# Packed matrix products recorded as one unit, and a mode-change charge in the order of the work

## The chip, the cores and the metric

One core of a Trainium2 chip runs the whole program. Its engines are TensorE (PE in the profile, PEld its weight loads), VectorE (DVE), ScalarE (ACT), GpSimdE (POOL, idle here) and SyncE (SP), which issues the transfers. The metric is the device time of one execution in microseconds (us), the median of several runs.

## What is computed

Two models one after the other on 256 tokens of width 1024, all in fp32, for one sequence. Cut to the parts around the change:

```python
def mixer_layer(...):                       # first block, 2 layers
    proj = h @ w_in
    ...                                     # 4 diff heads, 6 dilated heads, 6 forgetting heads
    s = einsum('bhmqd,bhmkd->bhmqk', qblk, k) * scale      # diff: two maps m per head, 32 wide
    p = softmax(where(causal, s, -inf))
    a = p[:, :, 0] - lam * p[:, :, 1]
    oa = einsum('bhqk,bhkd->bhqd', a, v)
    ...
def hybrid_layer(...):                      # second block, 2 layers
    ...                                     # 6 neighbourhood heads, 6 latent (MLA) heads, a convolution
    x = x + expert_choice_moe(rms_norm(x, norm_ffn), ...)
def expert_choice_moe(...):                 # 16 experts, 32 tokens each
    hid = silu(xs @ w_gate) * (xs @ w_up)
    ys = (hid @ w_down) * gate
    return zeros.at[bidx, idx].add(ys)
```

Each layer of the first block also has six modulation vectors (silu(c) @ w_mod), an output projection and a gated feed-forward stage with a width-3 convolution.

## The kernel before, in words

**Order of the work.** Nothing is issued where it is written. Every engine call is recorded by `Program.note` and `record` (lines 182 to 255) as one operation with its operands, a cost in ns (`cost`, 155) and its dependences. `order` (378) then makes a list schedule: `schedule` (257) keeps a list of ready operations per engine, sorted by rank, and again and again issues the one that can start first; of those that can start at the same time, the one of lower rank. Six forward rounds alternate with backward ones, and the round with the smallest modelled makespan is issued by `issue` (404), line 409: that is why every row of the profile names L409, and why rows are told apart by tile names. All operations that go through `either` (187) may run on VectorE or ScalarE, as the schedule finds better. Transfers keep their recorded order.

**The TensorE model.** For an operation on PE `record` notes its lanes, the 32-column strips of the array that its output covers (lines 211 to 213). An operation starts no earlier than its lanes are free; it then blocks its own lanes for its cost, and the engine itself for 20 ns. So the model knows that products in different column strips run side by side. It knows nothing of rows: two products that use different halves of the array's rows cover all four strips, and stand one behind the other in the model. Nor does it know any price for going from one shape of array use to another.

**Weights.** All weights stream through a ring of 16 buffers of 1 MiB (`ring`), filled by SP in one fixed sequence; a buffer is refilled when its last reader is done. A dense projection (`proj`, 801) splits each 512 weight columns into a rounded part (`whi`) and a rest (`wlo`) on VectorE or ScalarE, and takes three single-pass products for each 128x128 block: `ps<-h,whi` twice, `ps<-h,wlo` once. Everything else is plain fp32, which takes two passes: one product stands in the trace as two MATMUL records.

**Small products.** These do not fill the array:

- `modulation` (940): for each of 8 blocks k, four products of 32 output rows each, `ps<-ring,sct 128*32`. Seven of the twelve modulations run on VectorE instead (`ON_VECTOR`).
- `causal_scores` (988): for two query blocks b and two maps i, contraction over 64 rows, `ps<-kb,kb 64*128`. The forgetting heads add a row product with `pick6`.
- `attend` (1021): the probabilities are transposed on TensorE, then multiplied by the values of one or two heads, 64 output rows each, `ps<-kb,kb 128*64`.
- `soft_pair` (1257): the same for neighbourhood heads (64 rows) and latent heads (full rows).
- the experts (1575 to 1617): gate, up and down products of 32 output rows in groups of four, `ps<-ring,kb 128*32`, and eight products that scatter the result back, contraction over 32 rows, `ps<-kb,kb 32*128`, into four accumulators `yj`.

In the diff attention of `first_layer` (lines 1107 to 1126) the two maps passed to one `causal_scores` are those of the same head: q[0] and q[1] and the key all lie on partitions p0 to p0+63, with the other map's half zeroed. `attend` is called for one head at a time, with an offset that selects the half of `po`.

PSUM has eight buffers, all under the tag `ps`; the scores, sums, transposes and accumulators share them.

Of the kernel before, what the change touches and what calls it, by code (L numbers as in the profile page):

```python
# [21 lines left out]
NE = 16  # L22
# [16 lines left out]
class View:  # L39
    """A tile, or a view of one, that is allocated when the first instruction on it is issued."""  # L40
# [67 lines left out]
class Chunk:  # L108
    """Columns of a weight matrix that lie in several tiles."""
# [26 lines left out]
class Program:  # L136
    """Records instructions in the order of the data flow and issues them in the order in which a list
    scheduler finds their operands ready and their buffers free; the recorded order is the priority."""
# [5 lines left out]
    ROUNDS, PREFER, WAIT = 6, 3000.0, 1.0  # L144

    def __init__(self):
        self.ops, self.bufs, self.options = [], {}, None
        self.exp_ops, self.silu_ops, self.load, self.patience = [], [], None, 0.0

# [44 lines left out]
    def record(self, options):  # L194
        op = Op(index=len(self.ops), users={}, options={}, patience=self.patience)
        for engine, call, name, args, kw in options:
# [9 lines left out]
            op.options[engine] = call, args, kw, self.cost(engine, name, outs, ins, kw)  # L206
        op.engine = engine if len(options) == 1 else None
        op.cost, op.lag = min(o[3] for o in op.options.values()), max(self.LAG[e] for e in op.options)
        if engine == "PE":
            m = outs[0].shape[0]  # L210
            m = 32 if m <= 32 else 64 if m <= 64 else 128
            op.lanes = [0, 1, 2, 3][outs[0].part // m * m // 32:][:m // 32]
            op.columns = math.prod(outs[0].shape[1:]) * ins[0].shape[0] / 128 * len(op.lanes) / 4 * (
                2 if name == "transpose" else 1 if ins[0].dt == F32R else 4)
# [12 lines left out]
        func = args[2] if name == "activation" and op.engine else None  # L227
# [29 lines left out]
    def schedule(self, ops, rank, back=False):  # L257
        """A list schedule of the instructions, of which ops is an order that the buffers allow, or one
        of the reversed program."""
# [38 lines left out]
        lane = [0.0] * 4  # L298
        oldest, out = 0, []
        while len(out) < count:  # L300
# [3 lines left out]
            for e, ready in engines.items():  # L304
                found, tried = None, 0
                for r, i in ready:
# [39 lines left out]
            if e == "PE":  # L346
# [4 lines left out]
                columns += o.columns  # L351
            end = clock[e] = t + cost
# [50 lines left out]

    def issue(self):
        def real(a):
            return a.get() if isinstance(a, View) else a

        for o in self.order():
            o.ins = o.call(*[real(a) for a in o.args], **{k: real(v) for k, v in o.kw.items()})  # L409
# [251 lines left out]
def hybrid_kernel(ctx: ExitStack, tc: tile.TileContext, A, out, taps=None):  # L661
# [278 lines left out]
    def modulation(l, r):  # L940
# [15 lines left out]
        for k in range(8):  # L956
            for j in range(4):
# [30 lines left out]
    def causal_scores(q, k, mask, fneg=None, ftok=None, heads=None):  # L988
        sp = [sps(), sps()]
        for b in (1, 0):  # L990
            n = 128 * (b + 1)
            o = 128 * b
            for i in range(2):
                PE.matmul(sp[i][:, o:o + n], q[i][:, b * 128:(b + 1) * 128], k[i][:, :n],
                          start=True, stop=fneg is None)
            if fneg is not None:
                for i in range(2):
                    s = slice(64 * i, 64 * i + 38)
                    PE.matmul(sp[i][:, o:o + n], pick6[s, heads + i:heads + i + 1].to_broadcast([38, 128]),
                              fneg[s, :n], start=False, stop=True)  # L1000
# [20 lines left out]
    def attend(maps, vs, po, off=0):  # L1021
        parts = []
        for i, (full, low) in enumerate(maps):
# [7 lines left out]
            parts.append((slice(off + 64 * i, off + 64 * i + 64), t0, t1))  # L1031
# [28 lines left out]
    def first_layer(l, squares, following):  # L1060
# [46 lines left out]
        for c in range(2):  # L1107
            po = ops()[:, :256]
            for hh in range(2):
                p0 = 64 * hh  # L1110
                q = [qk[c][m][p0:p0 + 64] for m in range(2)]
                k = [qk[2 + c][p0:p0 + 64]] * 2
                dst, r4 = causal_scores(q, k, cf[:, C_CAU:C_CAU + 256])
                V.tensor_scalar(r4[:, 1:4:2], r4[:, 1:4:2], lam[:, l:l + 1], None, op0=ALU.mult)
                for b in range(2):
                    a0, a1 = dst[2 * b][0], dst[2 * b + 1][0]
                    scaled(a0, a0, r4[:, 2 * b:2 * b + 1])
                    V.scalar_tensor_tensor(a0, a1, r4[:, 2 * b + 1:2 * b + 2], a0, op0=ALU.mult, op1=ALU.add)
                attend([(dst[2][0], dst[0][0])], lambda b, i: vhead(2 * c + hh)(b, 0), po, p0)
# [137 lines left out]
    def soft_pair(q, k, v, bias, rq=None):  # L1257
        sp = [sps(), sps()]
        for b in range(2):
            for i in range(2):  # L1260
                PE.matmul(sp[i][:, b * 256:(b + 1) * 256], q[i][:, b * 128:(b + 1) * 128], k[i],
                          start=True, stop=True)
# [33 lines left out]
        for j in range(2):  # L1296
            for i in range(2):
                PE.matmul(po[64 * i:64 * i + 64, :], v(j, i), pT[i][j], start=(j == 0), stop=(j == 1))
# [13 lines left out]
    def second_layer(l, squares):  # L1312
# [262 lines left out]
        for e in range(NE):  # L1575
# [6 lines left out]
            for h, wx in enumerate((wg, wu)):  # L1582
                for k in range(8):
                    for j in range(4):
                        o = k * 1024 + j * 256
                        PE.matmul(gu[32 * j:32 * j + 32, h * 256:(h + 1) * 256], xe[k], wx[:, o:o + 256],
                                  start=(k == 0), stop=(k == 7))
# [17 lines left out]
            for kk in range(8):  # L1605
                for j in range(4):
                    o = kk * 1024 + j * 256
                    PE.matmul(po[32 * j:32 * j + 32, :256],
                              hT[:, (kk % 2) * 128 + 32 * (kk // 2):(kk % 2) * 128 + 32 * (kk // 2) + 32],
                              wd[:, o:o + 256], start=(kk == 0), stop=(kk == 7))  # L1610
            ys = kb()
            copy(ys, po[:, :256])
            for j in range(4):
                for c in range(2):
                    PE.matmul(yj[j][:, c * 256:(c + 1) * 256], ys[32 * j:32 * j + 32, c * 128:(c + 1) * 128],
                              gT[32 * j:32 * j + 32], start=(e == 0 and c == 0), stop=(e == NE - 1 and c == 1),
                              skip_group_check=True)
# [33 lines left out]
```

## Time and profile before

| | us |
|---|---|
| runs | 1908.0, 1904.19, 1908.54 |
| median of the runs | 1908.0 |
| profiled execution, first to last instruction (span) | 1906.3 |
| median above the span | 1.7 |

The page gives no other time for the profiled execution than its span. Read it by stages: the first block runs from 0 to about 706 us, the mixer of the second block's first layer from there to 857, its experts to 1299, the second layer's mixer to 1457, its experts to the end.

### The profile page before, as it was taken

To read this page: it belongs to the slowest core of one execution; us is meant where nothing else is said; L and a number is where in the kernel's file an instruction comes from. 1 tells how busy PE (TensorE), PEld (TensorE's weight loads), DVE (VectorE), ACT (ScalarE), POOL (GpSimd) and SP (SyncE) were. 2 spreads that over 40 slices of the span, in tenths; PEclk is the share of its full clock that TensorE was granted. 3 is DMA by queue.
4 is the path that set the end of the run, shared out by engine and by line. 5 is a ranking of instruction groups with operands and counts; after the bars stand their busy time and mean duration, and the time that the engine had idled before them with its cause. 6 is when DMAs were issued, how large, how long until landed. Compare 5 with 4: busy or idle time off the path is not lost.

```text
span 1906.3 us, 34712 instructions
## 1 busy us (share of the span) xinstructions
PE 1648.6 (86%) x14238; PEld 1180.9 (62%) x14238; DVE 843.6 (44%) x2229; ACT 636.9 (33%) x1569; POOL 0.2 (0%) x4
## 2 busy tenths in 40 slices
PE   7999999999999999989787777688998887767676
PEld 5788999978899998775333332236786433222222
DVE  4889998777786885781000000005675001000000
ACT  4776554566554465742000000004563100000000
POOL 0000000000000000000000000000000000000000
PEclk7999999999999999989767778768999867788777
DMA  9969885633355443439999999999446999999997
GB/s 392 420 236 403 310 339 208 238 144 132 110 194 188 169 177 133 143 143 374 421 421 420 421 421 420 421 420 420 165 149 238 421 421 420 420 422 420 421 421 326
DMA packets 88142, 594.95 MB, mean 312 GB/s; under 512 B 9904, under 2 KB 13616, under 8 KB 20784
## 3 DMA queue, kind: packets, MB, share of 16 engines
q1 hardware_dynamic: 87984, 592.75, 77.5%
q8 instruction: 111, 1.82, 0.4%
q14 instruction: 47, 0.39, 0.1%
HBM read 591.66 MB, written 1.05 MB: 311 GB/s over the span
## 4 chain that ended last, share of the span: by engine, by line
PE 54%; DMA 41%; DVE 3%; ACT 1%; issue 1%; SPq 0%; DVEq 0%; ACTq 0%
PE ps L409 54%; DMA ring<-in_ring_dram 41%; DVE kb L409 1%; ACT kb L409 1%; DVE wlo L409 0%; DVE h L409 0%; DVE ti L409 0%; DVE x L409 0%; ACT whi L409 0%; SPq L409 0%; ACT ti L409 0%; ACT h L409 0%; DVE aff L409 0%; DVE whi L409 0%; DVE sel L409 0%
## 5 line engine op out<-in xcount | busy, mean ns | idle before, releaser
L409 PE MATMUL ps<-ring,kb 128*32 128x256 f32 (+1 forms) x6024 | 501.7, 473 | 169.2 <-DMA ring<-in_ring_dram 159.2
L409 PEld LDWEIGHTS ps<-ring,kb 128*32 128x32 f32 (+1 forms) x6024 | 195.5, 129 | 442.5 <-DMA ring<-in_ring_dram 246.7
L409 PE MATMUL ps<-h,whi 128*128 128x256 f32 x2944 | 463.4, 290 | 5.2 <-DVE h L409 5.1
L409 PEld LDWEIGHTS ps<-h,whi 128*128 128x128 f32 x2944 | 407.4, 193 | 16.1 <-issue 8.2
L409 DVE TENSOR_TENSOR wlo<-ring,whi 128x512 fp32r<-128x512 f32 (+1 forms) x512 | 337.4, 675 | 87.8 <-PE ps L409 43.5
L409 DVE TENSOR_TENSOR kb<-kb,ps 128x256 f32<-128x256 f32 x76 | 31.7, 417 | 751.9 <-ACT kb L409 751.9
L409 ACT CAST whi<-ring 128x512 fp32r<-128x512 f32 (+1 forms) x396 | 238.4, 608 | 206.6 <-PE ps L409 192.9
L409 PE MATMUL ps<-h,wlo 128*128 128x256 f32 x1472 | 266.5, 286 | 0.0
L409 ACT ACTIVATE kb<-ps 32x256 f32<-32x256 f32 (+5 forms) x183 | 69.1, 379 | 570.7 <-PE ps L409 562.0
L409 PE MATMUL ps<-kb,kb 32*128 32x256 f32 (+6 forms) x1036 | 229.3, 458 | 13.4 <-ACT kb L409 8.8
L409 PEld LDWEIGHTS ps<-h,wlo 128*128 128x128 f32 x1472 | 220.1, 190 | 4.9 <-issue 3.4
L409 ACT COPY kb<-ps 128x256 f32<-128x256 f32 (+1 forms) x230 | 78.8, 360 | 352.9 <-PE ps L409 345.9
L409 PEld LDWEIGHTS ps<-kb,kb 32*128 32x128 f32 (+4 forms) x1036 | 121.9, 203 | 108.1 <-issue 62.0
L409 PE MATMUL ps<-cm,kb 128*128 128x128 f32 (+2 forms) x514 | 87.3, 285 | 48.1 <-DVE kb L409 46.3
L409 PEld LDWEIGHTS ps<-cm,kb 128*128 128x128 f32 (+1 forms) x514 | 66.2, 166 | 83.7 <-DVE kb L409 53.0
L409 PE MATMUL ps<-kb,whi 128*128 128x256 f32 x704 | 117.4, 281 | 0.0
L409 PEld LDWEIGHTS ps<-kb,whi 128*128 128x128 f32 x704 | 102.4, 188 | 0.0
L409 ACT ACTIVATE kb<-kb,ti 128x256 f32<-128x256 f32 (+1 forms) x176 | 76.7, 464 | 7.5 <-DVE ti L409 7.5
L409 PE MATMUL ps<-kb,wlo 128*128 128x256 f32 x352 | 77.7, 282 | 0.0
L409 DVE CAST whi<-ring 128x512 fp32r<-128x512 f32 (+1 forms) x116 | 48.6, 421 | 40.3 <-PE ps L409 32.7
L409 PE MATMUL ps<-whi,h 128*128 128x512 f32 (+1 forms) x192 | 62.0, 394 | 0.0
L409 PEld LDWEIGHTS ps<-kb,wlo 128*128 128x128 f32 x352 | 60.8, 188 | 0.0
(161 smaller groups left out, 1059.0 us busy)
## 6 DMA issues: line engine op xcount, KB each, us to landing
ring<-in_ring_dram SPq DMA_DIRECT2D x520, 1024.0 KB, 19.8
ring<-in_ring_dram SPq DMA_DIRECT2D x20, 960.0 KB, 5.6
ring<-in_ring_dram SPq DMA_DIRECT2D x8, 896.0 KB, 4.6
ring<-in_ring_dram SPq DMA_DIRECT2D x8, 512.0 KB, 18.1
spare<-in_ring_dram SPq DMA_DIRECT2D x12, 256.0 KB, 5.2
kb<-in_ring_dram SPq DMA_DIRECT2D x22, 128.0 KB, 3.1
cst<-in_nb_dram SPq DMA_DIRECT2D x2, 1152.0 KB, 11.4
cst<-in_ring_dram SPq DMA_DIRECT2D x2, 1024.0 KB, 7.3
```

The costliest lines, as they stand in the source:

```text
L409: o.ins = o.call(*[real(a) for a in o.args], **{k: real(v) for k, v in o.kw.items()})
```

## The change

Calls recorded inside `with prog.together():` become one operation. It is issued whole, its calls one behind the other; it waits for all operands of all calls, and needs all its buffers at once. Its modelled cost is a table of 4x4 cells of the array: each call adds its cost to the cells that it covers, and the fullest cell counts. Each PE operation has a mode (how many row strips and column strips one call covers), and an operation whose mode differs from that of the one issued last starts no earlier than the end of all lanes plus `SWITCH`, 95 ns. Two costs of the model change: a transfer from 360 to 421 bytes per ns, a single-pass product from n / 2.4 + 3 to n * 0.4515 + 4. The units are: one block k of a modulation (4 calls), all scores of a pair (4 calls, 8 in the forgetting heads), the value products of a pair (4), the scores of `soft_pair` (4) and its value products (4), each group of four in the experts, and the eight scatter products, now with c outside and j inside. In the diff attention one `causal_scores` call now takes one map of two heads, on partitions 0 to 63 and 64 to 127, and `attend` takes both heads.

```diff
+    SWITCH = 95.0
@@ cost
-            return v.shape[0] * free(v) * 4 / 360.0
+            return v.shape[0] * free(v) * 4 / 421.0
-                return n / 2.4 + 3
+                return n * 0.4515 + 4
+    @contextmanager
+    def together(self):
+        self.joint = []
+        yield
+        calls, self.joint = self.joint, None
+        self.record(calls, True)
+
     def note(self, *option):
+        if self.joint is not None:
+            return self.joint.append(option)
+    @staticmethod
+    def array(outs, ins):
+        m, k, r, c = outs[0].shape[0], ins[0].shape[0], ins[0].part // 32, outs[0].part // 32
+        k = 1 if k <= 32 else 2 if k <= 64 else 4
+        m = 1 if m == 32 else 2 if m == 64 else 4
+        return range(r // k * k, r // k * k + k), range(c // m * m, c // m * m + m)
@@ record, for every call of a unit
+                op.mode, op.lanes = (len(r), len(c)), list(c)
+                place = np.ix_(list(r), list(c))
+                cells[place] = cells[place].max() + cost
+                if joint:
+                    op.lanes, cost = [0, 1, 2, 3], cells.max()
+                    call, args, kw, outs, ins = self.in_turn, [list(calls)], {}, all_outs, all_ins
@@ schedule
+                    if e == "PE" and o.mode != mode:
+                        t = max(t, max(lane) + self.SWITCH)
...
+                mode = o.mode
@@ attend
-        for i, (o, t0, t1) in enumerate(parts):
-            PE.matmul(po[o, :], vs(0, i), t0, start=True, stop=False)
-        for i, (o, t0, t1) in enumerate(parts):
-            PE.matmul(po[o, 128:256], vs(1, i), t1[:, :128], start=False, stop=True)
+        with prog.together():
+            for i, (o, t0, t1) in enumerate(parts):
+                PE.matmul(po[o, :], vs(0, i), t0, start=True, stop=False)
+            for i, (o, t0, t1) in enumerate(parts):
+                PE.matmul(po[o, 128:256], vs(1, i), t1[:, :128], start=False, stop=True)
@@ first_layer
-            for hh in range(2):
-                p0 = 64 * hh
-                q = [qk[c][m][p0:p0 + 64] for m in range(2)]
-                k = [qk[2 + c][p0:p0 + 64]] * 2
-                dst, r4 = causal_scores(q, k, cf[:, C_CAU:C_CAU + 256])
-                V.tensor_scalar(r4[:, 1:4:2], r4[:, 1:4:2], lam[:, l:l + 1], None, op0=ALU.mult)
-                for b in range(2):
-                    a0, a1 = dst[2 * b][0], dst[2 * b + 1][0]
-                    scaled(a0, a0, r4[:, 2 * b:2 * b + 1])
-                    V.scalar_tensor_tensor(a0, a1, r4[:, 2 * b + 1:2 * b + 2], a0, op0=ALU.mult, op1=ALU.add)
-                attend([(dst[2][0], dst[0][0])], lambda b, i: vhead(2 * c + hh)(b, 0), po, p0)
+            k = [qk[2 + c][64 * i:64 * i + 64] for i in range(2)]
+            (dst, r4), (dst1, r41) = [causal_scores([qk[c][m][64 * i:64 * i + 64] for i in range(2)], k,
+                                                    cf[:, C_CAU:C_CAU + 256]) for m in range(2)]
+            V.tensor_scalar(r41, r41, lam[:, l:l + 1], None, op0=ALU.mult)
+            for n in range(4):
+                a0, a1 = dst[n][0], dst1[n][0]
+                scaled(a0, a0, r4[:, n:n + 1])
+                V.scalar_tensor_tensor(a0, a1, r41[:, n:n + 1], a0, op0=ALU.mult, op1=ALU.add)
+            attend([(dst[2 + i][0], dst[i][0]) for i in range(2)], vhead(2 * c), po)
@@ experts
-            for j in range(4):
+            with prog.together():
                 for c in range(2):
-                    PE.matmul(yj[j][:, c * 256:(c + 1) * 256], ...
+                    for j in range(4):
+                        PE.matmul(yj[j][:, c * 256:(c + 1) * 256], ...
```

The other units wrap existing loops in `with prog.together():` and change nothing in them. `issue` calls `in_turn`, which runs the calls of a unit one after another.

## Rows read from the trace of the kernel before

**Rows 1.** The page: busy time by engine, and the chain that ended last.

```profile
PE 1648.6 (86%) x14238; PEld 1180.9 (62%) x14238; DVE 843.6 (44%) x2229; ACT 636.9 (33%) x1569; POOL 0.2 (0%) x4
...
PE 54%; DMA 41%; DVE 3%; ACT 1%; issue 1%; SPq 0%; DVEq 0%; ACTq 0%
```

**Rows 2.** Stages: length, busy us (x instructions) of each engine, granted clock, DMA share, GB/s.

```profile
30.00:180.00 150.00, 145.02 (x1067) 121.20 (x1066) 132.01 (x433) 107.46 (x307) 0.00 (x0) 0.95 0.88 356
180.00:375.00 195.00, 194.52 (x1656) 191.82 (x1654) 173.68 (x399) 101.53 (x196) 0.00 (x0) 1.00 0.74 277
375.00:515.00 140.00, 133.09 (x926) 115.25 (x926) 104.37 (x319) 90.73 (x254) 0.00 (x0) 0.97 0.41 149
...
740.00:861.00 121.00, 113.33 (x748) 94.51 (x748) 89.78 (x255) 69.89 (x191) 0.00 (x0) 0.94 0.36 130
...
893.00:1299.00 406.00, 309.34 (x2923) 134.95 (x2924) 17.80 (x50) 20.20 (x52) 0.00 (x0) 0.75 1.01 421
1299.00:1461.00 162.00, 149.29 (x996) 127.39 (x989) 115.45 (x310) 92.32 (x248) 0.00 (x0) 0.93 0.56 218
```

**Rows 3.** Groups by shape, PE alone, 30 to 180 us: busy us, mean ns.

```profile
L409 PE MATMUL ps<-kb,kb 64*128 64x256 f32 x40 | 11.2, 474 | 2.3 <-DVE kb L409 2.3
...
L409 PE MATMUL ps<-ring,sct 128*32 128x256 f32 x128 | 8.4, 384 | 0.0
L409 PE MATMUL ps<-kb,kb 128*64 128x256 f32 x32 | 6.5, 405 | 0.0
L409 PE MATMUL ps<-kb,kb 64*128 64x128 f32 x40 | 6.1, 302 | 0.0
```

**Rows 4.** Timeline of PE, second mixer: a score product issued alone (start, length, records).

```profile
1352.26 0.34 PE L409 MATMUL ps<-wlo,h 128*128 128x384 f32 x1
1352.44 0.34 PE L409 MATMUL ps<-whi,h 128*128 128x384 f32 x1
1352.70 0.70 PE L409 MATMUL ps<-kb,kb 64*128 64x256 f32 x2
1353.33 0.45 PE L409 MATMUL ps<-whi,h 128*128 128x384 f32 x1
```

**Rows 5.** Timeline, second mixer: four score products issued together.

```profile
1385.19 0.74 PEld L409 LDWEIGHTS ps<-kb,kb 64*128 64x128 f32 x8 [0.33 <-ACT ti L409]
...
1386.27 0.51 PE L409 MATMUL ps<-h,whi 128*128 128x256 f32 x2
```

**Rows 6.** Timeline of PE, second mixer: four value products.

```profile
1392.25 1.08 PE L409 MATMUL ps<-kb,kb 128*64 128x256 f32 x8
1393.26 0.92 PE L409 MATMUL ps<-kb,ring 128*128 128x256 f32 x3
```

**Rows 7.** Groups by shape, PE alone, 1299 to 1457 us.

```profile
L409 PE MATMUL ps<-kb,kb 128*64 128x256 f32 x48 | 8.4, 396 | 0.0
...
L409 PE MATMUL ps<-kb,kb 64*128 64x256 f32 x24 | 6.4, 415 | 0.0
```

**Rows 8.** Timeline of PE, first expert stage.

```profile
1001.51 1.13 PE L409 MATMUL ps<-kb,kb 32*128 32x256 f32 x8
1002.57 1.07 PE L409 MATMUL ps<-ring,kb 128*32 128x256 f32 x16
```

**Rows 9.** Timelines of PE and SP where the first expert stage begins.

```profile
857.08 2.08 PE L409 MATMUL ps<-kb,h 128*128 128x256 f32 x8 [0.74 <-DVE kb L409]
...
860.85 4.82 SPq L409 DMA_DIRECT2D ring<-in_ring_dram  x3
```

**Rows 10.** Groups by shape, VectorE, 30 to 180 us.

```profile
L409 DVE CUSTOM_DVE_ANT_0 ring<-ring,cst 128x768 f32<-128x768 f32 x32 | 29.8, 948 | 0.0
...
L409 DVE CUSTOM_DVE_ANT_0 kb<-ps,cst 128x256 f32<-128x256 f32 x20 | 7.9, 421 | 1.4 <-PE ps L409 1.3
```

**Rows 11.** Groups by shape, whole span: the exponentials, and copies out of PSUM.

```profile
L409 ACT ACTIVATE kb<-kb,ti 128x256 f32<-128x256 f32 x114 | 55.5, 500 | 6.6 <-DVE ti L409 6.5
...
L409 ACT COPY kb<-ps 128x256 f32<-128x256 f32 x199 | 72.5, 373 | 350.4 <-PE ps L409 345.7 <-DVE kb L409 2.2
```

More of the change, by code (lines that the diff above doesn't have):

```diff
@@ L1 @@
 import math
-from contextlib import ExitStack
+from contextlib import ExitStack, contextmanager
 import numpy as np
@@ L148, in __init__ @@
         self.exp_ops, self.silu_ops, self.load, self.patience = [], [], None, 0.0
+        self.joint = None
     def tile(self, pool, shape, dt, name, tag, bufs):
@@ L192, in either, with record @@
         return self.record(options)
-    def record(self, options):
+    @staticmethod
[4 more added lines that the diff above has]
+        return range(r // k * k, r // k * k + k), range(c // m * m, c // m * m + m)
+    def record(self, options, joint=False):
         op = Op(index=len(self.ops), users={}, options={}, patience=self.patience)
+        all_outs, all_ins, calls, columns = [], [], [], 0.0
+        cells = np.zeros((4, 4))
         for engine, call, name, args, kw in options:
@@ L205, in record @@
                     (outs if k == "accum_out" else ins).append(v)
-            op.options[engine] = call, args, kw, self.cost(engine, name, outs, ins, kw)
-        op.engine = engine if len(options) == 1 else None
-        op.cost, op.lag = min(o[3] for o in op.options.values()), max(self.LAG[e] for e in op.options)
[L209 to L214, printed above, removed]
+            cost = self.cost(engine, name, outs, ins, kw)
+            if engine == "PE":
+                r, c = self.array(outs, ins)
+                op.mode, op.lanes = (len(r), len(c)), list(c)
+                columns += math.prod(outs[0].shape[1:]) * ins[0].shape[0] / 128 * len(c) / 4 * (
+                    2 if name == "transpose" else 1 if ins[0].dt == F32R else 4)
+                place = np.ix_(list(r), list(c))
+                cells[place] = cells[place].max() + cost
+                calls.append((call, args, kw))
+                all_outs += outs
+                all_ins += ins
+                op.columns = columns
+                if joint:
+                    op.lanes, cost = [0, 1, 2, 3], cells.max()
+                    call, args, kw, outs, ins = self.in_turn, [list(calls)], {}, all_outs, all_ins
+            op.options[engine] = call, args, kw, cost
+        op.engine = engine if joint or len(options) == 1 else None
+        op.cost, op.lag = min(o[3] for o in op.options.values()), max(self.LAG[e] for e in op.options)
         deps = {}
@@ L226, in record @@
                 dep(o, False)
-        func = args[2] if name == "activation" and op.engine else None
+        func = args[2] if name == "activation" and op.engine and not joint else None
         if name == "preload_act_table_set":
@@ L297, in schedule @@
         hot, columns, tick = False, 0.0, 0.0
-        lane = [0.0] * 4
+        lane, mode = [0.0] * 4, None
         oldest, out = 0, []
@@ L402, in order, with real, in_turn @@
         return [o for o, _ in best[1]]
+    @staticmethod
+    def real(a):
+        return a.get() if isinstance(a, View) else a
+    def in_turn(self, calls):
+        for call, args, kw in calls:
+            call(*[self.real(a) for a in args], **{k: self.real(v) for k, v in kw.items()})
     def issue(self):
-        def real(a):
-            return a.get() if isinstance(a, View) else a
         for o in self.order():
-            o.ins = o.call(*[real(a) for a in o.args], **{k: real(v) for k, v in o.kw.items()})
+            o.call(*[self.real(a) for a in o.args], **{k: self.real(v) for k, v in o.kw.items()})
 def lam_init(layer):
@@ L989, in causal_scores @@
         sp = [sps(), sps()]
[L990 to L996, printed above, removed]
-                for i in range(2):
-                    s = slice(64 * i, 64 * i + 38)
-                    PE.matmul(sp[i][:, o:o + n], pick6[s, heads + i:heads + i + 1].to_broadcast([38, 128]),
-                              fneg[s, :n], start=False, stop=True)
+        with prog.together():
+            for b in (1, 0):
+                n = 128 * (b + 1)
+                o = 128 * b
+                for i in range(2):
+                    PE.matmul(sp[i][:, o:o + n], q[i][:, b * 128:(b + 1) * 128], k[i][:, :n],
+                              start=True, stop=fneg is None)
+                if fneg is not None:
+                    for i in range(2):
+                        s = slice(64 * i, 64 * i + 38)
+                        PE.matmul(sp[i][:, o:o + n], pick6[s, heads + i:heads + i + 1].to_broadcast([38, 128]),
+                                  fneg[s, :n], start=False, stop=True)
         pa, pb_, pc = kb(), kb(), kb()
@@ L1019, in causal_scores, with attend @@
         return dst, r4
-    def attend(maps, vs, po, off=0):
+    def attend(maps, vs, po):
         parts = []
@@ L1030, in attend @@
             copy(t1[:, :128], tp[:, 256:384])
-            parts.append((slice(off + 64 * i, off + 64 * i + 64), t0, t1))
-        for i, (o, t0, t1) in enumerate(parts):
-            PE.matmul(po[o, :], vs(0, i), t0, start=True, stop=False)
-        for i, (o, t0, t1) in enumerate(parts):
-            PE.matmul(po[o, 128:256], vs(1, i), t1[:, :128], start=False, stop=True)
+            parts.append((slice(64 * i, 64 * i + 64), t0, t1))
+        with prog.together():
+            for i, (o, t0, t1) in enumerate(parts):
+                PE.matmul(po[o, :], vs(0, i), t0, start=True, stop=False)
+            for i, (o, t0, t1) in enumerate(parts):
+                PE.matmul(po[o, 128:256], vs(1, i), t1[:, :128], start=False, stop=True)
     def split_f32(dst_h, dst_l, src):
@@ L1258, in soft_pair @@
         sp = [sps(), sps()]
[L1259 to L1262, printed above, removed]
+        with prog.together():
+            for b in range(2):
+                for i in range(2):
+                    PE.matmul(sp[i][:, b * 256:(b + 1) * 256], q[i][:, b * 128:(b + 1) * 128], k[i],
+                              start=True, stop=True)
         nb, s4, r4 = tiny(4), tiny(4), tiny(4)
@@ L1295, in soft_pair @@
             copy(pT[i][1], tp[:, 256:])
-        for j in range(2):
-            for i in range(2):
-                PE.matmul(po[64 * i:64 * i + 64, :], v(j, i), pT[i][j], start=(j == 0), stop=(j == 1))
+        with prog.together():
+            for j in range(2):
+                for i in range(2):
+                    PE.matmul(po[64 * i:64 * i + 64, :], v(j, i), pT[i][j], start=(j == 0), stop=(j == 1))
         o = kb()
@@ L1583, in second_layer @@
                 for k in range(8):
-                    for j in range(4):
-                        o = k * 1024 + j * 256
-                        PE.matmul(gu[32 * j:32 * j + 32, h * 256:(h + 1) * 256], xe[k], wx[:, o:o + 256],
-                                  start=(k == 0), stop=(k == 7))
+                    with prog.together():
+                        for j in range(4):
+                            o = k * 1024 + j * 256
+                            PE.matmul(gu[32 * j:32 * j + 32, h * 256:(h + 1) * 256], xe[k], wx[:, o:o + 256],
+                                      start=(k == 0), stop=(k == 7))
             sg = kb()
@@ L1605, in second_layer @@
             for kk in range(8):
[L1606 to L1610, printed above, removed]
+                with prog.together():
+                    for j in range(4):
+                        o = kk * 1024 + j * 256
+                        PE.matmul(po[32 * j:32 * j + 32, :256],
+                                  hT[:, (kk % 2) * 128 + 32 * (kk // 2):(kk % 2) * 128 + 32 * (kk // 2) + 32],
+                                  wd[:, o:o + 256], start=(kk == 0), stop=(kk == 7))
             ys = kb()
             copy(ys, po[:, :256])
-            for j in range(4):
+            with prog.together():
                 for c in range(2):
-                    PE.matmul(yj[j][:, c * 256:(c + 1) * 256], ys[32 * j:32 * j + 32, c * 128:(c + 1) * 128],
-                              gT[32 * j:32 * j + 32], start=(e == 0 and c == 0), stop=(e == NE - 1 and c == 1),
-                              skip_group_check=True)
+                    for j in range(4):
+                        PE.matmul(yj[j][:, c * 256:(c + 1) * 256], ys[32 * j:32 * j + 32, c * 128:(c + 1) * 128],
+                                  gT[32 * j:32 * j + 32], start=(e == 0 and c == 0), stop=(e == NE - 1 and c == 1),
+                                  skip_group_check=True)
         log_exp_set()
```

## The prediction, made before the changed kernel ran

> **What bounds the kernel now.** I read the page first. TensorE is busy 86% of the span, and the chain that ended last runs over TensorE for 54% and over transfers for 41% [rows 1]; a mean over two kinds of stage. The table by stages parts them [rows 2]. In the expert stage from 893 to 1299 us the transfers are at 1.01 of their share and 421 GB/s, while TensorE is busy 309 of 406 us: what TensorE saves there is worth nothing (the second expert stage looks the same). In the two first layers and both mixers it is the other way: TensorE is busy 133 to 145 us of 140 to 150, and the transfers are mostly below their limit. Only there, in some 700 us, can the change pay, and a microsecond saved there moves everything behind it, since the expert stages follow with a fixed length of their own. Between the layers' attentions (180 to 375 us) TensorE is full with dense products alone and nothing changes.
>
> One reservation stands in the same table: in the first layer VectorE is busy 132.0 of 150 us, in the second 104.4 of 140, in the mixers about 90 of 121 and 115 of 162 [rows 2]. In the first layer it carries modulations besides, 29.8 us in their long pieces alone [rows 10].
>
> **What a packed product costs.** I then looked at single runs. A 64-row score product issued alone between dense ones takes 0.63 us to the next start (1352.70 to 1353.33), and the step into it is 0.26 us where the same kind of dense product before had 0.18: 0.08 more [rows 4]. Four such products issued together, in pairs on the two row halves, take 1.08 us (1385.19 to 1386.27) [rows 5]. So four alone cost 4 x 0.71 = 2.84 us and a unit of four 1.16 us. Four value products in two column halves take 1.01 us [rows 6]; they are two products long on each half, and each is two passes. That the array runs both halves side by side is thus shown for rows and for columns; the kernel of before only gets it by luck, because its model doesn't know of rows and may put a dense product into the middle of a group.
>
> **The change, part by part.** Units count to the next start, groups by their busy time, which holds a tail of 0.07 us a run (0.70 against 0.63 [rows 4]); I add it to the units, so 1.08 becomes 1.15.
>
> Scores, mixers. 24 records, 12 products, 6.4 us now [rows 7]; after, 3 units of 1.15 us, 3.45. The twelve stand in eight runs now, so five steps of 0.08 go as well. Saved 3.3 us in the second mixer; the first has the same 24 records, so 6.6 in both.
>
> Scores, layers. Ten calls a layer (four diff, three dilated, three forgetting). The 40 + 40 records take 11.2 + 6.1 = 17.3 us [rows 3]. A unit is two passes of 256 and two of 128 columns: the 1.15 us less two half passes of 0.11 is 0.93, ten make 9.3. Of the 8.0 between I take off 2.0, because the two widths adjoin within a run and both count their tails: 6.0 a layer, 12.0 in both. The diff heads are the larger part of it: their two maps lie on the same rows today and cannot overlap at all, so pairing by head is what makes four units out of four serial calls.
>
> Value products. In a mixer 48 records take 8.4 us [rows 7], six units of 1.08 are 6.5 [rows 6]; some already run beside other products of the same mode, so I take 1.2 of the 1.9, 2.4 in both mixers. In a layer 32 long records take 6.5 us [rows 3]; eight units of two, 0.61 us each (half of 1.08 and the tail), are 4.9: 1.6, and 0.3 for the short ones, 3.8 in both layers. Pairing the diff heads is in this too.
>
> Modulations. 128 records take 8.4 us [rows 3]; groups of sixteen take 1.01 us where nothing cuts in (from 1002.57, the row of the experts; its 1.07 less the tail) [rows 8], so 8.0 or 8.1. With the mode steps that vanish I take 1.0 in the first layer and 0.5 behind it, 1.5.
>
> Experts. Eight records of the scatter take 1.06 us now (1001.51 to 1002.57), the sixteen of a weight tile 1.01 [rows 8]. Four row strips side by side would take three quarters off the first. Worth nothing: the transfers cover it [rows 2]. Without that cover it would be about 1.6 us an expert, which has sixteen such records.
>
> VectorE loses one tiny scaling for each pair of diff heads, four in all; its products, exponentials, transposes and copies stay in number and size. Nothing: VectorE's own queue hides it. SP's queue is not reordered, transfers keep their sequence; the two new cost figures move no work by themselves, they only redraw the order.
>
> Gross sum: 12.0 + 6.6 + 3.8 + 2.4 + 1.5 = 26.3 us; by stage 8.9, 8.4, 4.5 and 4.5.
>
> **What comes back.** In the first layer VectorE has 18 us idle in 150; squeezing 8.9 out leaves it 9 in 141, so much of the gain will wait for it. I count 40% there, 80% elsewhere: 3.6 + 13.9 = 17.5. Next, a unit waits for both heads and for two PSUM buffers at once, and the mode charge lets a dense product that is ready go first. No row of before shows such a wait; the part not counted, 8.8 us, is what I leave for it, with 0 as its lower bound and the softmax chain below as its upper one.
>
> Last, the restart of the transfers at each expert stage. The ring is full there, SP issues again at 860.85 when the first expert's tile is read, after eight gather products in 2.0 us of slow clock [rows 9]. There are 32 gather products; if the charge keeps the other 24 ahead of the first expert, at 0.12 us a product (195 us for 1656 records in the dense stretch [rows 2]) the restart is 2.9 us later, twice. Bounds 0 and 5.8, I take 1.5, nearer the end at which it stands now. Net saving 16.0 us.
>
> Against the profiled execution: 1906.3 - 16.0 = 1890.3. The median of the runs is 1.7 above that span, so 1892.
>
> Two rules of the Trainium skill speak against this size. Rows 5 show pairs overlapping almost wholly. TensorE: Matmul & The Clock Gate, Part 3 (Measured speedup vs the span model), gives 3.07 for packing four row strips where four would be ideal. As an estimate from that page, a unit's 0.86 us of passes would be 1.12, about 5.6 us less over 26 units, and the time 1896. The same part says that weight loads overlap running products only where the row groups differ. By that, value products and modulations would gain nothing, 7.7 us less, and the time would be 1897; the trace disagrees, since sixteen four-strip records on the same rows take 1.01 us [rows 8].
>
> **The rivals.** First, the saved TensorE time turns into waits for softmax and VectorE. For it: VectorE's share in the first layer [rows 2]. Against it: TensorE's waits for VectorE in that layer are 2.3 us in its costliest group [rows 3], and ScalarE, idle 42 us of 150, can take copies. If the layers give nothing and the mixers half, 4.5 less 1.5 is 3 us: 1905.
>
> Second, slower. The mode charge makes the list schedule prefer any ready dense product, whatever its rank, so scores and values are put off to the end of each attention stage, where no dense work is left to run beside their softmax. One pair's chain is four reductions (0.42 us for the long ones [rows 10]), four exponentials (0.50 [rows 11]) with their sums, scaling, transposes, two copies of 0.37 [rows 11] and the values, about 7 us; two pairs at once about 10, as ScalarE is then in series. Four stages with 10 us exposed are 40 against 26 saved: 14 slower, 1922. It decides from 6.6 us exposed in each stage. Against it: the backward rounds pull late chains forward, and the model does see these chains.
>
> Third, the new order also removes stalls that I don't count (each of the many short runs also breaks the dense stream): the whole 26 and up to 10 more, 1872. That the change does nothing of what it says is hardly possible, since rows 4 and 5 show both states; its share is in the first rival.
>
> **How the numbers follow.** My forecast, 1876 to 1900, has 0.60; the first rival (1900 to 1908) 0.17; the slower one 0.15, a fifth of it just above 1908; the third 0.08. A measurement here tells 0.3%, 5.7 us, from no change. Faster by more: 0.60 + 0.08 and 0.06 of the first rival, 0.74. Within: 0.11 and 0.03 of the slower case, 0.14. Slower: 0.12. The range 1870 to 1912 holds the forecast, the first rival, most of the third and the beginning of the slower case, and leaves out under 0.2.
>
> **What would show it.** Right: 64-row score records in runs of 8 in the mixers, pairs a few ns apart, 0.93 us a call in the layers; the first expert tile read about 10 us earlier than now, the second stage's some 14; expert stages as long as before, with TensorE less busy. The steps are wrong if the short groups' busy time falls by 20 us or more and the stages do not shorten (first rival), or if TensorE shows idle stretches of several us before the output projections (second). SP issuing later after the last score product than 2 us would show the restart.

## The result: slower by 0.7%

The changed kernel took 1922.07 us (median of 4 runs, 1919.54 to 1922.92) against 1908.27 for the kernel before: ratio 1.0071, 95% interval [1.0057, 1.0086]. Its profiled execution spans 1920.9 us, 14.6 more than before. The forecast of 1892 and its range were wrong, in direction too.

**The page after** shows less work and more time. The lines answer to [rows 1].

```profile
PE 1536.9 (80%) x14238; PEld 1136.7 (59%) x14238; DVE 850.3 (44%) x2266; ACT 622.7 (32%) x1528; POOL 0.2 (0%) x4
...
DMA 43%; PE 27%; DVE 5%; ACT 1%; issue 1%; SPq 0%; DVEq 0%; ACTq 0%
```

The number of matrix records is the same, their busy time 112 us lower, and the chain has half as much TensorE in it. Most of the 112 us lies where it is worth nothing: the scatter products of the experts (`ps<-kb,kb 32*128`) alone went from 137.7 to 44.5 us, beside transfers that took as long as before. Groups by shape, TensorE alone, 30 to 180 us; they answer to [rows 3]:

```profile
L444 PE MATMUL ps<-kb,kb 64*128 64x256 f32 x40 | 8.7, 477 | 0.0
...
L444 PE MATMUL ps<-ring,sct 128*32 128x256 f32 x128 | 7.3, 380 | 0.0
L444 PE MATMUL ps<-kb,kb 128*64 128x256 f32 x32 | 5.5, 424 | 0.0
L444 PE MATMUL ps<-kb,kb 64*128 64x128 f32 x40 | 5.3, 300 | 0.0
```

The same view from 1299 to 1470 us, the second mixer; it answers to [rows 7]:

```profile
L444 PE MATMUL ps<-kb,kb 128*64 128x256 f32 x48 | 7.9, 410 | 0.0
...
L444 PE MATMUL ps<-kb,kb 64*128 64x256 f32 x24 | 3.5, 398 | 0.0
```

The short products got cheaper: the mixer's scores went from 6.4 to 3.5 us (3.45 forecast), its values from 8.4 to 7.9 (a saving of 0.5 where 1.2 was forecast), the first layer's scores from 17.3 to 14.0 (both widths together, where 11.3 was forecast). So the packing works, and the time went elsewhere. The timeline of TensorE in the first layer shows where (start, length, records, idle before and its releaser):

```profile
104.37 0.64 PE L448 MATMUL ps<-h,wlo 128*128 128x256 f32 x4
104.93 1.58 PE L444 MATMUL ps<-kb,kb 64*128 64x256 f32 x16
108.44 3.35 PE L448 MATMUL ps<-h,kb 128*12 128x256 f32 x16 [1.93 <-DVE ti L448]
111.72 1.13 PE L444 MATMUL ps<-kb,kb 64*128 64x256 f32 x8
116.17 1.95 PE L448 MATMUL ps<-cm,kb 128*128 128x128 f32 x6 [3.32 <-DVE kb L448]
118.05 4.41 PE L444 MATMUL ps<-kb,kb 64*128 64x256 f32 x24
```

The first score of the layer starts at 104.93 us. Before, it started at 49.31, and scores, values and dense products alternated until 140. Now TensorE issues 347 records between these two times, and all of them belong to dense products; before, 82 of the 314 in the same stretch belonged to others. Then the scores come in heaps, and TensorE waits 1.93 and 3.32 us for VectorE, with its granted clock down to 0.67 (between 110 and 120 us), that is for the greater part at the lower of its levels (1.2 GHz, not 2.4). The first mixer shows the whole softmax chain uncovered:

```profile
812.75 0.42 DVE L448 CUSTOM_DVE_ANT_0 kb<-ps,cst 128x256 f32<-128x256 f32 x1
...
813.89 0.51 ACT L448 ACTIVATE kb<-kb,ti 128x256 f32<-128x256 f32 x1 [1.13 <-DVE ti L448]
...
815.38 0.49 ACT L448 ACTIVATE kb<-kb,ti 128x256 f32<-128x256 f32 x1
...
816.00 0.18 DVE L448 RECIPROCAL ti<-ti 128x4 f32<-128x4 f32 x1
...
816.62 2.02 PE L448 MATMUL ps<-cm,kb 128*128 128x128 f32 x8 [4.30 <-DVE kb L448]
```

Reductions, exponentials and the reciprocal follow one another, and TensorE stands idle for 4.30 us until the scaled probabilities can be transposed; the next stretch (815 to 825 us) again has a granted clock of 0.66. Over the whole first mixer (745 to 868 us) the granted clock is 0.92; in the kernel before (740 to 857 us) it is 0.96. The third place is where the experts begin; it answers to [rows 9]. TensorE's timeline first:

```profile
867.93 6.91 PE L448 MATMUL ps<-kb,h 128*128 128x256 f32 x36 [0.74 <-DVE kb L448]
874.77 2.58 PE L444 MATMUL ps<-ring,kb 128*32 128x256 f32 x44
```

and SP's, in which the next two transfers are issued:

```profile
875.90 1.19 SPq L448 DMA_DIRECT2D ring<-in_ring_dram  x2
```

All 32 products of the first gather and four of the second now precede the first expert tile, 6.84 us instead of 2.01, and the transfers restart 8.0 us behind the gather's start instead of 3.8.

**The ledger**, in us. It cuts both timelines at the starts of the gather, of the first expert product and of the token rows (`ps<-cm,ti`, the short products that spread a norm's factor for each token over the partitions; a norm begins with them):

| piece | before | after | difference |
|---|---|---|---|
| to the token rows behind the first layer's attention | 176.0 | 181.7 | +5.7 |
| to those at the second layer's start | 196.1 | 205.0 | +8.9 |
| to those behind its attention | 139.5 | 132.9 | -6.6 |
| to the first gather | 345.5 | 348.3 | +2.8 |
| to the first expert product | 2.0 | 6.8 | +4.8 |
| to the second gather | 598.2 | 593.4 | -4.8 |
| to the first expert product | 2.0 | 7.1 | +5.1 |
| to the end | 447.1 | 445.7 | -1.4 |

The same difference by kind says more. I take TensorE from 30 us to the first gather, and from the first stage's last scatter to the second gather, that is, everything but the start and the expert stages. There its busy time fell from 952.2 to 927.3 us, and its idle time rose from 32.8 to 64.8. So 24.9 us of work went and 32.0 us of waiting came; the two restarts add 9.9, and the expert stages themselves give back 2.4. Together that is the 14.6 us.

### The profile page after: what moved, and what is told of

Same layout as the page of the kernel before. It is cut to its first block, busy times and chain, and to the rows that moved or that the text cites. A ratio compares the mean times of both kernels' runs of the same rounds, so it can differ in the third digit from the quotient of the medians.

```text
span 1920.9 us, 34766 instructions
## 1 busy us (share of the span) xinstructions
PE 1536.9 (80%) x14238; PEld 1136.7 (59%) x14238; DVE 850.3 (44%) x2266; ACT 622.7 (32%) x1528; POOL 0.2 (0%) x4
## 4 chain that ended last, share of the span: by engine, by line
DMA 43%; PE 27%; DVE 5%; ACT 1%; issue 1%; SPq 0%; DVEq 0%; ACTq 0%
DMA ring<-in_ring_dram 43%; PE ps L448 24%; PE ps L444 3%; DVE kb L448 3%; ACT kb L448 1%; DVE wlo L448 1%; DVE ti L448 1%; DVE x L448 0%; DVE h L448 0%; ACT h L448 0%; ACT whi L448 0%; DVE whi L448 0%; ACT ti L448 0%; DVE aff L448 0%; DVE sel L448 0%
## 5 line engine op out<-in xcount | busy, mean ns | idle before, releaser
L444 PE MATMUL ps<-ring,kb 128*32 128x256 f32 x6016 | 492.9, 466 | 263.4 <-DMA ring<-in_ring_dram 250.6
L444 PEld LDWEIGHTS ps<-ring,kb 128*32 128x32 f32 x6016 | 189.9, 128 | 551.8 <-DMA ring<-in_ring_dram 398.1
L448 PE MATMUL ps<-h,whi 128*128 128x256 f32 x2944 | 453.6, 288 | 10.3 <-DVE h L448 8.9
L448 ACT ACTIVATE kb<-ps 32x256 f32<-32x256 f32 (+4 forms) x181 | 67.2, 378 | 569.5 <-PE ps L444 552.9
L448 ACT COPY kb<-ps 128x256 f32<-128x256 f32 (+1 forms) x209 | 72.3, 364 | 337.1 <-PE ps L444 246.2
L444 PE MATMUL ps<-kb,kb 32*128 32x256 f32 (+6 forms) x1036 | 115.3, 432 | 9.9 <-ACT kb L448 9.7
L444 PEld LDWEIGHTS ps<-kb,kb 32*128 32x128 f32 (+4 forms) x1036 | 75.6, 199 | 41.7 <-ACT kb L448 22.5
L448 ACT ACTIVATE kb<-kb,ti 128x256 f32<-128x256 f32 (+1 forms) x155 | 68.1, 460 | 11.8 <-DVE ti L448 11.6
L448 DVE TENSOR_TENSOR kb<-kb,kb 128x256 f32<-128x256 f32 (+2 forms) x144 | 59.2, 420 | 1.6 <-ACT kb L448 0.3
L448 DVE COPY kb<-ps 128x256 f32<-128x256 f32 (+2 forms) x94 | 36.1, 398 | 53.5 <-ACT kb L448 50.3
```

What stands on the lines that cost most here:

```text
L444: call(*[self.real(a) for a in args], **{k: self.real(v) for k, v in kw.items()})
L448: o.call(*[self.real(a) for a in o.args], **{k: self.real(v) for k, v in o.kw.items()})
```

## The experiments

Theory 1: the mode charge makes the schedule prefer any ready dense product, whatever its rank. Rivals: theory 2, the units do the harm by waiting for all operands and buffers at once; theory 3, VectorE bounds the first layer whatever the order. Ratios below are against runs of the kernel before on the same chip. Three chips were used, on which the kernel before took 1907.4 to 1909.0 us; two runs from different chips are therefore best compared by their ratios. "Idle time" is that of TensorE, counted as under the ledger.

**No charge.** `SWITCH = 95.0` becomes `0.0`.

> The changed kernel with the mode charge set from 95 to 0 ns; units, pairing of the diff heads and new cost figures stay. Theory 1 (the charge lets every ready dense product go ahead of the small ones, whatever their rank): the first score of the first layer comes back from 104.9 us to near 49, the first expert tile follows the gather's start by 2 us instead of 7, and the time falls to 1885 to 1900 us. Theory 2 (the units themselves are the harm: they wait for all operands and for several PSUM buffers at once): scores still late, 1915 us or more. Theory 3 (VectorE bounds the first layer whatever the order): scores early, but the first layer no shorter than before; 1900 to 1912 us.

Measured 1899.33 us, ratio 0.9952 [0.9936, 0.9969]. The first score starts at 48.55 us, and the timeline at the gather (TensorE) is like that of before [rows 9]:

```profile
849.48 2.08 PE L448 MATMUL ps<-kb,h 128*128 128x256 f32 x8 [0.74 <-DVE kb L448]
851.49 1.94 PE L444 MATMUL ps<-ring,kb 128*32 128x256 f32 x16
853.35 1.82 PE L448 MATMUL ps<-kb,h 128*128 128x256 f32 x8
```

The charge costs 22.7 us here. By the same ledger, 9.7 of it lie in the first layer, 8.3 between the second layer's token rows and the gather, 9.9 in the two restarts, of which 4.9 come back later; the other pieces differ by under 1 us. TensorE's busy time is the same (927.5 us), its idle time 46.4 instead of 64.8: the charge makes waits, not work. But the time is at the slow end of the forecast: the piece behind the first layer is 205.4 us long, no shorter than with the charge.

**No units.** In `together` the calls are no longer gathered: `yield` alone.

> The changed kernel with every call recorded by itself again; the mode charge, the pairing and the new cost figures stay. Theory 1: first score near 105 us still, all gather products before the first expert tile, 1915 to 1930 us. Theory 2: scores back near 49 us, at most 1908 us. Theory 3: about 1915 us, without a statement on the first score.

1917.43 us, 1.0050 [1.0033, 1.0066]; first score at 105.0, first expert 7.0 us behind the gather, idle time 61.9. Theory 2 falls: without units the harm stays.

**Old cost figures.** `421.0` back to `360.0`, `n * 0.4515 + 4` back to `n / 2.4 + 3`.

> The changed kernel with the two cost figures of before (360 bytes per ns, n / 2.4 + 3). Theories 1 to 3: no part in it, within 6 us of 1922. If the new figures are what moved the order: 1900 us or less.

1915.66 us, 1.0037 [1.0024, 1.0050]: 6.4 less, just past the 6 expected; late scores stay (103.4).

**No pairing.** The diff attention of before.

> The changed kernel with the diff attention of before, two maps of one head in one call. It undoes the pairing alone. Theory 1: scores still start near 105 us, and the serial maps cost 2 to 6 us more TensorE time, 1922 to 1930 us. If the pairing were the harm (it makes both maps of two heads wait for each other): 1910 us or less.

1927.78 us, 1.0104 [1.0089, 1.0119]: the pairing is worth 5.7 us, as expected.

**Rank first.** The charge stays in the modelled time, but may not overturn the rank:

```diff
-  if found is None or t + o.patience * o.options[e][3] < found[0] - self.SLACK:
+  if found is None or t + o.patience * o.options[e][3] < found[0] - (100.0 if e == "PE" else self.SLACK):
```

> The changed kernel with the charge kept at 95 ns, but on TensorE an operation of lower priority goes first only if it can start over 100 ns earlier, so that the charge alone cannot overturn the rank. Theory 1 in its strict form (the harm is that the charge overturns the rank): first score near 50 us, 1890 to 1903 us. If the harm is that the modelled 95 ns themselves mislead the order (theory 1 in a loose form): scores late again, 1912 us or more.

1895.45 us, 0.9933 [0.9918, 0.9948]. Timeline of TensorE:

```profile
47.20 0.86 PE L448 MATMUL ps<-whi,h 128*128 128x512 f32 x3
48.15 0.93 PE L444 MATMUL ps<-kb,kb 64*128 64x256 f32 x8
49.00 0.73 PE L448 MATMUL ps<-wlo,h 128*128 128x512 f32 x2
```

This settles theory 1 in its strict form: with the same 95 ns in the model the scores are early again, and the idle time is 41.4 us. (The 100 ns hold for every choice on TensorE, not only for changes of mode, and were not run without the charge; so the time of this run alone does not price the charge.) The row also gives the unit's price, 0.85 us from start to start; forecast was 0.93 with a tail of 0.07.

**Charge in the experts alone.** An operation carries its charge: 95 from the gather to the end of each expert stage, 0 elsewhere.

> The charge only for what is recorded from the gather to the end of each expert stage, 0 elsewhere. Theory 1, by place: the first expert tile follows the gather's start by 7 us instead of 2 in both layers, everything else as without a charge: 1899 + 10 = 1909 us. If the charge does its harm in the attention stages alone: 1897 to 1902 us.

1899.84 us, 0.9955 [0.9940, 0.9970]. The first restart moved as expected, to 7.1 us (the second to 6.2):

```profile
846.38 7.19 PE L448 MATMUL ps<-kb,h 128*128 128x256 f32 x36 [0.74 <-DVE kb L448]
853.50 2.80 PE L444 MATMUL ps<-ring,kb 128*32 128x256 f32 x48
```

but the 10 us did not appear. From the first expert product to the stage's last scatter it took 438.7 us against 441.2 without a charge, so half the delay came back, and the front happened to be 3 us shorter. A miss of size, not of place.

**No charge, old figures.** Both edits above together.

> No charge and the two cost figures of before; the units and the pairing alone. If the new cost figures lengthen the dense stretch behind the first layer (205 us against 196 before), that stretch is back at 196 to 198 us and the time is 1888 to 1894 us. If VectorE's backlog from the shortened first layer lengthens it, the stretch stays at 202 us or more and the time at 1896 to 1902 us.

1888.85 us, 0.9897 [0.9882, 0.9912]. The piece behind the first layer is 197.3 us (170.30 to 367.58). Theory 3 is refuted as a bound: 197 us is possible right behind a first layer that ended 5.7 us earlier than before.

**No charge, no pairing.**

> No charge, diff heads unpaired, the rest as changed. The worth of the pairing alone beside the run without a charge: by the prediction's rows the four serial calls of a layer cost about 1.6 us each instead of 0.9 and the values somewhat more, 3 to 4 us a layer, so 1903 to 1907 us. If VectorE or the order decides there, within 3 us of 1899.

1903.10 us, 0.9965 [0.9951, 0.9980], 3.8 above the run with pairing, as expected; but the two intervals overlap, so this pair alone does not show it.

**One new figure at a time**, without a charge: transfers, then products.

> No charge, the old figure for single-pass products, the new one for transfers (421). Of the 10.5 us between no charge with old figures (1888.9) and with new ones (1899.3) this gives the transfers' part. If it is the transfers' figure: 1897 to 1901. If it is the products' figure: 1887 to 1891. If both figures are harmless and the 10.5 us are only the luck of another order: neither this nor the run with the other figure alone need lie between the two.

> No charge, the old figure for transfers, the new one for single-pass products (n * 0.4515 + 4). If the products' figure lengthens the stretch behind the first layer: 1897 to 1901. If it is the transfers' figure: 1887 to 1891.

1888.23 us, 0.9899 [0.9884, 0.9913], and 1886.83 us, 0.9891 [0.9876, 0.9906], the lowest median of all, though not clear of the run with the other figure or of the one with neither. Neither figure does harm alone.

**Luck of an order.** `LAG["PE"]` from 230 to 232 ns, first in the run without a charge, then in the kernel before.

> The run without a charge (new figures), with one modelled latency moved by 2 ns of 230, which has no meaning of its own: it only redraws the order. The luck of an order is the difference from 1899.3. If luck is small: 1897 to 1902. If luck alone can make the 10.5 us: outside 1893 to 1906.

1894.23 us, 0.9929 [0.9914, 0.9944]: 5.1 us from the run that it jitters, whose interval it just overlaps. The waits for VectorE in the piece behind the first layer were then 2.3 us for `ti` and 1.5 for `wlo`, against 2.2 and 2.0 without the jitter and none of either with the old figures.

> The kernel before with one modelled latency moved by 2 ns of 230: only the luck of its order. If luck is about 5 us either way, as between the runs without a charge: 1901 to 1914. If the order of before was a lucky one: 1914 or more.

1905.54 us, 0.9996 [0.9986, 1.0006]. No difference is shown: nothing speaks for a lucky or an unlucky order of before. From these two draws, which are few, I take about 5 us as what an order can make by luck.

**Rank first, old figures.**

> The charge kept, rank first on TensorE within 100 ns, the two old cost figures. If the old figures are worth 6 to 10 us whatever the charge does: 1885 to 1890, the fastest so far. If luck makes them: anywhere from 1888 to 1902.

1889.89 us, 0.9913 [0.9897, 0.9930], 5.6 below rank first with the new figures; the intervals overlap, so the old figures' worth is not shown here.

**The parts alone**, each with the old figures. In the first two there is no charge. Two small things of the change stay in all three: the scatter's loops keep their new order, and a product with fewer than 32 output rows counts in the model as covering all four column strips, where it was one.

> The pairing of the diff heads alone: no units, no charge, old cost figures. Four pairs of products a layer can now overlap where they are issued together by chance, and the model does not see it: 1900 to 1908. If the pairing needs the units to pay: within the luck of 1908.

1903.40 us, 0.9983 [0.9974, 0.9993]: less than luck by its size.

> The units alone: no pairing, no charge, old cost figures. By the rows of before the units carry most of the 26 us (all but 6 to 8 of them): 1890 to 1898. If they give nothing without the pairing: within the luck of 1908.

1899.35 us, 0.9962 [0.9949, 0.9974], 8 us, at the slow end and past it. Both together gave 20 us: 8 + 4 and some 8 more, as one would expect where only paired heads make a unit whose halves overlap; but 8 us is not far above luck, so that is not shown.

> The strict charge alone: no units, no pairing, old cost figures. Theory 1: the first score again near 105 us, all gather products before the first expert tile, 1918 to 1935 us. If the charge hurts only together with the units: within the luck of 1908.

1927.30 us, 1.0111 [1.0096, 1.0126]. First score at 105.14, and the gather whole:

```profile
867.81 6.49 PE L445 MATMUL ps<-kb,h 128*128 128x256 f32 x36 [0.74 <-DVE kb L445]
874.23 3.01 PE L445 MATMUL ps<-ring,kb 128*32 128x256 f32 x52
```

**Side by side**, the charge off and strictly on, in four settings (us):

| units, pairing, figures | off | on | charge |
|---|---|---|---|
| none, none, old | 1907.7 | 1927.3 | +19.6 |
| both, new | 1899.3 | 1922.1 | +22.7 |
| both, old | 1888.9 | 1915.7 | +26.8 |
| units alone, new | 1903.1 | 1927.8 | +24.7 |

Four times 20 to 27 us is far beyond the 5 us of luck and the 1.5 us between chips. In the first line "off" is the kernel before itself; the two small things that the run with the charge has besides are also in the run of the pairing alone, which took 1903.4. The idle times part the kernels in the same way: 61 to 65 us in the five with the strict charge everywhere, 33 to 46 in the other thirteen, the kernel before among them.

## Why the prediction was wrong

**What bounds the kernel: right.** (The stages in which the change can pay add up to 573 us, not "some 700", and in the mixers TensorE is busy 113 of 121 and 149 of 162 us, which I gave with the layers as one range [rows 2]; the sum uses neither.) The expert stages kept the length that transfers set: 893 to 1299 before, 908 to 1314 after, at 421 GB/s both times, while TensorE's busy time in them fell from 309 to 258 us [rows 2]; windows of 406 us each:

```profile
908.00:1314.00 406.00, 258.04 (x2904) 105.12 (x2896) 17.71 (x50) 18.18 (x46) 0.00 (x0) 0.79 1.01 421
```

**The price of the packed products: right in the sum.** Gross 26.3 us were forecast, and TensorE's busy time outside the expert stages fell by 24.9. A causal unit was forecast at 0.93 and takes 0.85 plus its tail; the mixer's scores were forecast at 3.45 and take 3.5; the first layer's scores take the forecast 11.3 where they come early (rank first, 7.2 + 4.1). The mixer's values gave less than forecast. The five runs with units and pairing but no charge (1886.8, 1888.2, 1888.9, 1894.2, 1899.3) scatter around the forecast 1892. The first of the two rules of the Trainium skill that I weighed (TensorE: Matmul & The Clock Gate, Part 3) I applied twice over: by its 3.07 instead of 4, as an estimate, the 0.86 us of passes become 1.12, but the 1.08 of [rows 5] already held nearly that, and I set the loss on top. So it asked for no 5.6 us more. The causal unit's row agrees by its number, since 0.65 us of passes times 4 / 3.07 is 0.85; but the loss is about 0.2 us in both units, which looks more like a fixed price than like a factor. The second fell already in the trace of before.

**What comes back: this is the step that failed.** For the waits that the mode charge makes I left 8.8 us, shared with VectorE. What the runs show in its place is 32.0 us more idle time of TensorE than before, and a charge that costs 20 to 27 us of time. Without the charge the idle time grows by 13.6 us, with the old figures by 6.6, so what I counted for VectorE was of the right size and the term of the charge was not. The mechanism was on paper as the second rival, with its sign, idle stretches of several us, and even with its time (1922), and I gave it 0.15 on the argument that "the backward rounds pull late chains forward, and the model does see these chains". They do not: in every run with the strict charge everywhere the first score of the first layer starts between 103.35 and 105.14 us. The code says why. While TensorE is free, all ready operations can start at the same time and the rank decides; with the charge a product of the running mode is always 95 ns earlier, so the tie, and with it the rank, is gone. As long as a dense product is ready no score is issued. I read `schedule` as a model of time and overlooked that its tie was the priority. The rival's price per place was off as well: I put 10 us into each of four attention stages, but it was 9.7 in the first layer, 8.3 by the first mixer, and next to nothing in the second layer and the second mixer (and in the run of the charge alone, against the kernel before, 12.5 in the first layer and none by the first mixer). That its 1922 was met is luck: it had 40 us of exposed chains and no restart, against 32.0 and 9.9.

**The restart: right in place, wrong in size.** Bounds 0 to 5.8, taken 1.5. The gather delayed the first expert by 4.8 and 5.1 us, since its 36 records run in part at the lower clock (granted 0.50 from 868 to 873 us; 6.84 us in all, 0.19 each, not 0.12); about half came back within the stage.

**The first rival** (VectorE takes the saving back) is not what happened, but it has a grain: the waits for `wlo` and `ti` behind the first layer are VectorE's, and they vary with the order. Of the 13.9 us between the spans of the runs at 1886.8 and 1899.3 that piece makes 6.1, and these waits 3.0 (1.2 against 4.2); the rest is spread over the other pieces.

**Open.** Three comparisons have both new figures together 5.6 to 10.5 us slower than the old ones (in the smallest the intervals overlap), while each alone does nothing. With 5 us of luck in an order I cannot say whether the pair is harmful; it was not tried with more orders. Whether 95 ns is a good charge when the rank is kept is open too: rank first and no charge lie within luck of each other (1889.9 and 1888.9 with old figures).

## What to carry to other kernels

In a greedy list schedule a small charge added to start times is not only a cost: where starts used to tie, it replaces the priority. Give such a charge a slack of its own size, then compare the position of the first critical operation, not only the modelled end. And before a few microseconds between two orders are explained, redraw one of them with a change that means nothing.

The version to keep is the units with the pairing of the diff heads and no charge: 1886.8 us with the new product figure, 0.9891 [0.9876, 0.9906], and as good within the noise with the old ones.

## What the runs showed of the hardware

Four score products on two row halves take 0.85 us where 0.65 is their bare passes (two of 256 and two of 128 columns, which follow one another 0.216 and 0.109 us apart where nothing cuts in); the other 0.2 us is about what a lone score product also takes over its passes (0.63 to the next start against 0.43 [rows 4]), so it looks like the way into and out of the mode, paid once a unit. TensorEngine Tiling (Array Packing) of the Trainium skill, Key Properties, says that changing the tiling mode drains the array. The trace agrees in so far as the change costs time: with the 0.08 us of the step into it, a lone product pays some 0.3 us over its passes [rows 4]. That is small beside what a schedule loses by avoiding it: one uncovered softmax chain is 4.3 us.
